# Deeper load buffers, stores held back, and arithmetic spread over three engines in a residual layer normalization

## The chip, the cores and the metric

The kernel runs on one core of a Trainium2 chip. The metric is the device time of one execution in microseconds (us). The profile names the core's engines: DVE is the vector engine, ACT the scalar engine, Pool the general engine, and SyncE (SP in the profile) only issues transfers here. "SPq", "POOLq" and "DVEq" are the queues or sequencers of those engines. DMA stands for the core's 16 transfer engines. The *span* is the time from the first to the last instruction in the profile; the time is about 1.7 to 2 us longer.

## The reference

```python
x, residual: (16, 1024, 512) float32; gamma, beta: (512,); eps = 1e-5

z = x + residual
mean = np.mean(z, axis=-1, keepdims=True)
var = np.var(z, axis=-1, keepdims=True)
return gamma * (z - mean) / np.sqrt(var + eps) + beta
```

There are 16384 rows of 512 numbers. With 128 rows to a tile that is 128 tiles. Two inputs of 33.55 MB are read and one output of 33.55 MB is written, and nothing is used twice, so nearly all of the 101.02 MB on the profile's page is unavoidable.

## The kernel before

The rows are worked on in 39 chunks: a head of 1, 1 and 2 tiles, 28 chunks of 4 tiles, and a tail of 2, 2, 2, 2, 1, 1, 1, 1 tiles. All loads are issued by SyncE and all stores by Pool, which also converts from fp16 to fp32. There are three buffers for X and three for R.

```python
LOAD_BUFS = 3
WORK_BUFS = 4
...
for ci, ns in enumerate(chunks):
    ...
    X = loads.tile([P, ns * D], FP32, name="X", tag="X")
    R = loads.tile([P, ns * D], FP32, name="R", tag="R")
    x_dma_eng.dma_start(out=X, in_=xs)                 # SyncE
    r_dma_eng.dma_start(out=R, in_=rs)                 # SyncE
    ...
    for j in range(ns):                                # Z = X + R, sz = its sum, on DVE
        nc.vector.tensor_tensor_reduce(out=Z3[:, j, :], in0=X3[:, j, :], in1=R3[:, j, :],
            ..., op0=OP.add, op1=OP.add, accum_out=sz[:, j : j + 1])
    for j in range(ns):                                # sq = sum of squares, on ACT
        nc.scalar.activation(out=sqd, in_=Z3[:, j, :], func=AF.Square,
            accum_out=sq[:, j : j + 1])
    nc.scalar.activation(out=msq, in_=sz, func=AF.Square, scale=inv_D)
    nc.vector.scalar_tensor_tensor(out=vr, in0=sq, scalar=inv_D, in1=msq, ...)
    nc.scalar.activation(out=rstd, in_=vr, func=AF.Sqrt, bias=eps_t)
    nc.vector.reciprocal(out=rstd, in_=rstd)
    nc.scalar.activation(out=nm, in_=sz, func=AF.Identity, scale=-inv_D)
    for j in range(ns):                                # normalize, times gamma, plus beta: all DVE
        nc.vector.tensor_scalar(out=W3[:, j, :], in0=Z3[:, j, :], scalar1=nm[...], scalar2=rstd[...], ...)
        nc.vector.tensor_tensor(out=W3[:, j, :], in0=W3[:, j, :], in1=gamma_b, op=OP.mult)
        nc.vector.tensor_tensor(out=W3[:, j, :], in0=W3[:, j, :], in1=beta_b, op=OP.add)
    nc.gpsimd.dma_start(out=os_, in_=W)                # Pool
```

## Time and profile before

| what | before |
|---|---|
| time, median of 16 runs | 256.96 us (256.57 to 258.44) |
| span of the profiled run | 255.1 us |
| DVE, ACT, Pool busy | 215.3, 106.4, 22.1 us |
| transfer rate, 20 to 215 us | 423 GB/s |
| bytes moved after 215 us | 11.98 MB in 40.1 us |

First the page of the kernel before. The line of digits gives DVE's busy share in tenths in 40 equal slices of the span, and the line below it the GB/s of those slices.

```profile
span 255.1 us, 1456 instructions
...
DVE 215.3 (84%) x720; ACT 106.4 (42%) x375; POOL 22.1 (9%) x45
...
DVE  1577799998889899778979878898887889999972
...
GB/s 148 399 421 416 421 425 423 425 424 421 423 425 418 429 420 424 425 421 424 420 423 429 420 424 424 421 429 419 425 427 421 423 426 385 407 384 403 347 129 123
...
```

The reader should see a flat middle at 420 to 425 GB/s in which DVE is *not* full (mostly 7 to 9 tenths), and then an end that falls off: the last two slices move 129 and 123 GB/s. The next fence is the table of stretches: start and end, length, the busy time of each engine (with the number of instructions), the granted clock, the DMA share and GB/s.

```profile
...
core 0: us, DVE busy (x) ACT busy (x) POOL busy (x), PEclk, DMA share, GB/s
20.00:215.00 195.00, 172.08 (x571) 82.31 (x286) 13.29 (x25) 1.00 1.09 423
215.00:240.00 25.00, 24.76 (x88) 13.19 (x50) 3.19 (x6) 1.00 1.04 380
240.00:244.10 4.10, 2.79 (x12) 2.30 (x10) 0.53 (x1) 1.00 0.87 307
244.10:255.10 11.00, 5.37 (x18) 1.39 (x6) 2.12 (x4) 1.00 0.39 111
...
```

From 20 to 215 us the transfers are the limit. From 215 to 240 us DVE is: it is busy for 24.76 of 25 us, and the rate falls to 380 GB/s. The waits of SyncE's queue from 215 to 245 us say what the loads wait for (what waited, on what; us in total, times, longest; L99 is line 99 of that kernel):

```profile
...
SPq L99 <- DVE W L144: 16.9, 5, 4.8
SPq L99 <- DVE sz L118: 9.9, 1, 9.9
SPq L99 <- DVE rstd L140: 1.8, 1, 1.8
```

The loads wait for DVE to free one of the three buffers. After the last load has landed (244.1 us), the rest is arithmetic on the last chunks and their stores, at 111 GB/s over 11 us.

### The profile page before, as it was taken

The page shows a single profiled execution, that of the slowest core. Times are in us where ns is not written, and L with a number is a line of the kernel's source. Part 1 is how long each engine was busy: PE and PEld are TensorE (multiplying, and loading weights), DVE is VectorE, ACT ScalarE, POOL GpSimd, SP SyncE. Part 2 cuts the span into 40 slices and gives each one's busy share as a digit, 9 for nine tenths or more (in the row PEclk, how much of TensorE's full clock was granted, in tenths as well). Part 3 has the DMA queues.
Part 4 walks back from the last instruction along what each step waited for, and adds up shares of the span by engine and source line. Part 5 has one row for each costly group of instructions (what it writes and reads, how often), then busy time and mean ns, then how long its engine had stood idle before and what let it go on. Part 6 is the DMA issues. An engine that isn't in the chain of part 4 may idle for free.

```text
span 255.1 us, 1456 instructions
## 1 busy us (share of the span) xinstructions
DVE 215.3 (84%) x720; ACT 106.4 (42%) x375; POOL 22.1 (9%) x45
## 2 busy tenths in 40 slices
DVE  1577799998889899778979878898887889999972
ACT  4133545352724335253332624334272333545530
POOL 2010000100000000000000000000000000011121
DMA  5999999999999999999999999999999999999944
GB/s 148 399 421 416 421 425 423 425 424 421 423 425 418 429 420 424 425 421 424 420 423 429 420 424 424 421 429 419 425 427 421 423 426 385 407 384 403 347 129 123
DMA packets 17147, 101.02 MB, mean 396 GB/s; under 512 B 1904, under 2 KB 2160, under 8 KB 6384
## 3 DMA queue, kind: packets, MB, share of 16 engines
q1 hardware_dynamic: 11232, 67.11, 68.7%
q0 software_dynamic: 5904, 33.82, 34.8%
q14 instruction: 11, 0.09, 0.1%
HBM read 67.63 MB, written 33.55 MB: 397 GB/s over the span
## 4 chain that ended last, share of the span: by engine, by line
DMA 52%; DVE 30%; issue 9%; ACT 5%; POOL 1%; SPq 1%; POOLq 0%; DVEq 0%; ACTq 0%
DMA R<-in_residual_dram 52%; DVE Z L118 10%; DVE W L144 7%; DVE W L152 6%; DVE W L155 5%; ACT sqd L129 4%; POOL out_dram L159 1%; SPq L99 1%; DVE rstd L140 1%; DVE sz L118 1%; DVE vr L136 1%; ACT rstd L139 0%; POOLq L192 0%; SPq L100 0%; ACT nm L141 0%
## 5 line engine op out<-in xcount | busy, mean ns | idle before, releaser
L129 ACT ACTIVATE sqd<-Z 128x512 f16<-128x512 f16 x128 | 79.7, 623 | 94.1 <-DVE sz L118 92.8
L118 DVE CUSTOM_DVE_ANT_0 Z<-X,R 128x512 f16<-128x512 f32 x128 | 84.4, 684 | 27.7 <-DMA R<-in_residual_dram 27.7
L152 DVE TENSOR_TENSOR W<-W,gamma_b 128x512 f16<-128x512 f16 x128 | 48.6, 422 | 0.1
L155 DVE TENSOR_TENSOR W<-W,beta_b 128x512 f16<-128x512 f16 x128 | 48.6, 422 | 0.1
L144 DVE TENSOR_SCALAR W<-Z,nm,rstd 128x512 f16<-128x512 f16 x128 | 47.3, 411 | 0.2
L159 POOL DMA_DIRECT2D out_dram<-W x39 | 20.7, 532 | 227.6 <-DVE vr L136 119.7
L139 ACT ACTIVATE rstd<-vr,eps_t 128x4 f32<-128x4 f32 (+2 forms) x39 | 11.3, 294 | 46.3 <-DVE vr L136 46.0
L129 ACT ACTIVATION_READ_ACCUMULATOR sqd<-Z 128x1 f32 x128 | 23.9, 186 | 0.0
L118 DVE DVE_READ_ACCUMULATOR2_ANT sz<- 128x1 f32 x128 | 10.9, 85 | 0.0
L136 DVE SCALAR_TENSOR_TENSOR vr<-sq,msq 128x4 f32<-128x4 f32 (+2 forms) x39 | 6.0, 159 | 4.5 <-ACT sqd L129 3.6
L140 DVE RECIPROCAL rstd<-rstd 128x4 f32<-128x4 f32 (+2 forms) x39 | 6.6, 171 | 1.4 <-ACT rstd L139 1.4
L135 ACT ACTIVATE msq<-sz 128x4 f32<-128x4 f32 (+2 forms) x39 | 7.4, 190 | 0.0
L141 ACT ACTIVATE nm<-sz 128x4 f32<-128x4 f32 (+2 forms) x39 | 7.3, 188 | 0.0
L88 ACT ACT_TABLE_LOAD x1 | 1.3, 1283 | 0.7 <-PEq L178 0.7
L85 DVE MEMSET eps_t<- 128x1 f32 x1 | 0.1, 59 | 0.8 <-PEq L178 0.8
L82 POOL DMA_DIRECT2D gamma_b<-in_gamma_dram x1 | 0.7, 667 | 0.8 <-PEq L192 0.8
L83 POOL DMA_DIRECT2D beta_b<-in_beta_dram x1 | 0.5, 540 | 0.0
L88 ACT ACTIVATE zero_t<-zero_t 128x1 f32<-128x1 f32 x1 | 0.2, 203 | 0.0
L178 POOL MEMSET const-float32-0.0<- 128x1 f32 x1 | 0.1, 98 | 0.2 <-issue 0.2
L178 POOL MEMSET const-bfloat16-1.0<- 128x1 bf16 x1 | 0.1, 101 | 0.0
L178 POOL MEMSET const-float32-1.0<- 128x1 f32 x1 | 0.1, 98 | 0.0
L178 POOL MEMSET const-uint8-127<- 128x1 uint8 x1 | 0.1, 98 | 0.0
(1 smaller groups left out, 0.1 us busy)
## 6 DMA issues: line engine op xcount, KB each, us to landing
X<-in_x_dram SPq DMA_DIRECT2D x28, 1024.0 KB, 11.4
R<-in_residual_dram SPq DMA_DIRECT2D x28, 1024.0 KB, 15.8
out_dram<-W POOLq DMA_DIRECT2D x28, 1024.0 KB, 9.3
X<-in_x_dram SPq DMA_DIRECT2D x5, 512.0 KB, 7.3
R<-in_residual_dram SPq DMA_DIRECT2D x5, 512.0 KB, 8.2
out_dram<-W POOLq DMA_DIRECT2D x5, 512.0 KB, 5.2
X<-in_x_dram SPq DMA_DIRECT2D x6, 256.0 KB, 5.1
R<-in_residual_dram SPq DMA_DIRECT2D x6, 256.0 KB, 5.4
```

The source lines that it names most:

```text
L99: x_dma_eng.dma_start(out=X, in_=xs)
L118: nc.vector.tensor_tensor_reduce(out=Z3[:, j, :], in0=X3[:, j, :], in1=R3[:, j, :], scale=1.0, scalar=0.0, op0=OP.add, op1=OP.add, accum_o ...
L129: nc.scalar.activation(out=sqd, in_=Z3[:, j, :], func=AF.Square, accum_out=sq[:, j : j + 1],)
L135: nc.scalar.activation(out=msq, in_=sz, func=AF.Square, scale=inv_D)
L136: nc.vector.scalar_tensor_tensor(out=vr, in0=sq, scalar=inv_D, in1=msq, op0=OP.mult, op1=OP.subtract)
L139: nc.scalar.activation(out=rstd, in_=vr, func=AF.Sqrt, bias=eps_t)
L140: nc.vector.reciprocal(out=rstd, in_=rstd)
L141: nc.scalar.activation(out=nm, in_=sz, func=AF.Identity, scale=-inv_D)
L144: nc.vector.tensor_scalar(out=W3[:, j, :], in0=Z3[:, j, :], scalar1=nm[:, j : j + 1], scalar2=rstd[:, j : j + 1], op0=OP.add, op1=OP.mult,)
L152: nc.vector.tensor_tensor(out=W3[:, j, :], in0=W3[:, j, :], in1=gamma_b, op=OP.mult)
L155: nc.vector.tensor_tensor(out=W3[:, j, :], in0=W3[:, j, :], in1=beta_b, op=OP.add)
L159: nc.gpsimd.dma_start(out=os_, in_=W)
```

## The change

Its intent is to keep the transfers full to the end. Three things change:

1. Six load buffers in place of three, so that loads need not wait for DVE.
2. Finished chunks are held back: up to five chunks stay in SBUF before their store is issued (`STORE_LAG = 5`, twelve W buffers). When the loads are done there are stores left to issue, and the arithmetic of the last chunks can run beside them.
3. Arithmetic is taken off DVE. The odd tiles of a chunk are normalized on ACT (61 of 128), and the statistics of the 31 head and bulk chunks are computed on Pool, with a power of -0.5 for the root. The order on DVE, ACT and Pool is written out by hand, with each chunk's second half after the first half of the next chunk.

The diff, cut to its core:

```diff
-LOAD_BUFS = 3
+LOAD_BUFS = 6
+W_BUFS = 12
+STORE_LAG = 5
+BULK_ON_POOL = True
+ZNORM = "split"
...
+        if on_pool:
+            nc.gpsimd.tensor_scalar(out=nm, in0=sz, scalar1=-inv_D, ..., op0=OP.mult)
+            nc.gpsimd.tensor_tensor(out=t0, in0=nm, in1=nm, op=OP.mult)
+            nc.gpsimd.tensor_scalar(out=t1, in0=sq, scalar1=inv_D, scalar2=eps, ...)
+            nc.gpsimd.tensor_tensor(out=t1, in0=t1, in1=t0, op=OP.subtract)
+            nc.gpsimd.tensor_tensor(out=rstd, in0=t1, in1=nhalf_t[:, :ns], op=OP.pow)
+            nc.gpsimd.tensor_tensor(out=bb, in0=nm, in1=rstd, op=OP.mult)
+        else:
+            nc.scalar.activation(out=t0, in_=sz, func=AF.Square, scale=inv_D)
+            # on Pool, so that the stores queued behind it keep pace with the loads
+            nc.gpsimd.tensor_scalar(out=nm, in0=sz, scalar1=-inv_D, ..., op0=OP.mult)
...
+    def stage_b_act(c):                      # odd tiles of a chunk
+            nc.scalar.activation(out=W3[:, j, :], in_=Z3[:, j, :], func=AF.Identity,
+                scale=rstd[:, j : j + 1], bias=bb[:, j : j + 1])
...
-        nc.gpsimd.dma_start(out=os_, in_=W)
+        for ci, ns in enumerate(chunks):
+            bulk = ci < n_bulk
+            full = len(held) >= (1 if bulk and BULK_ON_POOL else 2)
+            ...
+            new = stage_a(ns, bulk and BULK_ON_POOL)
+            ...
+            if full:
+                stage_b_dve(held.pop(0))
+            held.append(new)
+            store(max(0, len(pending) - STORE_LAG))
+        store(len(pending))
```

More of the change, by code (lines that the diff above doesn't have):

```diff
@@ L16 @@
 TAIL = [2, 2, 2, 2, 1, 1, 1, 1]
-LOAD_BUFS = 3
+LOAD_BUFS = 6
 WORK_BUFS = 4
-HALF = True
-X_DMA = "sync"
-R_DMA = "sync"
-OUT_DMA = "pool"
+W_BUFS = 12
+STORE_LAG = 5
+BULK_ON_POOL = True
+ZNORM = "split"
 @with_exitstack
@@ L65 @@
     assert sum(chunks) == n_tok_tiles
-    HT = FP16 if HALF else FP32
     consts = ctx.enter_context(tc.tile_pool(name="consts", bufs=1))
@@ L72 @@
     stats = ctx.enter_context(tc.tile_pool(name="stats", bufs=6))
-    dma_engines = {"act": nc.scalar, "sync": nc.sync, "pool": nc.gpsimd}
-    out_dma_eng = dma_engines[OUT_DMA]
-    x_dma_eng = dma_engines[X_DMA]
-    r_dma_eng = dma_engines[R_DMA]
-    gamma_b = consts.tile([P, D], HT)
-    beta_b = consts.tile([P, D], HT)
-    gb_load = nc.gpsimd if HALF else nc.sync
-    gb_load.dma_start(out=gamma_b, in_=gamma[None, :].to_broadcast((P, D)))
-    gb_load.dma_start(out=beta_b, in_=beta[None, :].to_broadcast((P, D)))
+    gamma_b = consts.tile([P, D], FP16)
+    beta_b = consts.tile([P, D], FP16)
+    nc.gpsimd.dma_start(out=gamma_b, in_=gamma[None, :].to_broadcast((P, D)))
+    nc.gpsimd.dma_start(out=beta_b, in_=beta[None, :].to_broadcast((P, D)))
     eps_t = consts.tile([P, 1], FP32)
@@ L87, with stage_a @@
     nc.vector.memset(zero_t, 0.0)
+    nhalf_t = consts.tile([P, NS_BULK], FP32)
+    nc.vector.memset(nhalf_t, -0.5)
     nc.scalar.activation(out=zero_t, in_=zero_t, func=AF.Sqrt)
     row0 = 0
-    for ci, ns in enumerate(chunks):
+    def stage_a(ns, on_pool):
+        nonlocal row0
         xs = xf[row0 : row0 + P * ns].rearrange("(p j) d -> p (j d)", j=ns)
@@ L98 @@
         R = loads.tile([P, ns * D], FP32, name="R", tag="R")
-        x_dma_eng.dma_start(out=X, in_=xs)
-        r_dma_eng.dma_start(out=R, in_=rs)
+        nc.sync.dma_start(out=X, in_=xs)
+        nc.sync.dma_start(out=R, in_=rs)
         X3 = X.rearrange("p (j d) -> p j d", d=D)
         R3 = R.rearrange("p (j d) -> p j d", d=D)
-        Z = work.tile([P, ns * D], HT, name="Z", tag="Z")
+        Z = work.tile([P, ns * D], FP16, name="Z", tag="Z")
         Z3 = Z.rearrange("p (j d) -> p j d", d=D)
-        W = work.tile([P, ns * D], HT, name="W", tag="W")
+        W = work.tile([P, ns * D], FP16, name="W", tag="W", bufs=W_BUFS)
         W3 = W.rearrange("p (j d) -> p j d", d=D)
-        sqd = work.tile([P, D], HT, name="sqd", tag="sqd", bufs=2)
+        sqd = work.tile([P, D], FP16, name="sqd", tag="sqd", bufs=2)
         sz = stats.tile([P, ns], FP32, name="sz", tag="sz")
         sq = stats.tile([P, ns], FP32, name="sq", tag="sq")
-        msq = stats.tile([P, ns], FP32, name="msq", tag="msq")
-        vr = stats.tile([P, ns], FP32, name="vr", tag="vr")
         rstd = stats.tile([P, ns], FP32, name="rstd", tag="rstd")
         nm = stats.tile([P, ns], FP32, name="nm", tag="nm")
+        bb = stats.tile([P, ns], FP32, name="bb", tag="bb")
+        t0 = stats.tile([P, ns], FP32, name="t0", tag="t0")
+        t1 = stats.tile([P, ns], FP32, name="t1", tag="t1")
         for j in range(ns):
@@ L134 @@
             )
-        nc.scalar.activation(out=msq, in_=sz, func=AF.Square, scale=inv_D)
-        nc.vector.scalar_tensor_tensor(
-            out=vr, in0=sq, scalar=inv_D, in1=msq, op0=OP.mult, op1=OP.subtract
-        )
-        nc.scalar.activation(out=rstd, in_=vr, func=AF.Sqrt, bias=eps_t)
-        nc.vector.reciprocal(out=rstd, in_=rstd)
-        nc.scalar.activation(out=nm, in_=sz, func=AF.Identity, scale=-inv_D)
-        for j in range(ns):
+        c = dict(ns=ns, W=W, W3=W3, Z3=Z3, nm=nm, rstd=rstd, bb=bb, os_=os_,
+                 t0=t0, t1=t1, sq=sq)
@@ new lines, in stage_a @@
+        if on_pool:
+            nc.gpsimd.tensor_scalar(
+                out=nm, in0=sz, scalar1=-inv_D, scalar2=None, op0=OP.mult
+            )
+            nc.gpsimd.tensor_tensor(out=t0, in0=nm, in1=nm, op=OP.mult)
+            nc.gpsimd.tensor_scalar(
+                out=t1, in0=sq, scalar1=inv_D, scalar2=eps, op0=OP.mult, op1=OP.add
+            )
+            nc.gpsimd.tensor_tensor(out=t1, in0=t1, in1=t0, op=OP.subtract)
[3 more added lines that the diff above has]
+            nc.scalar.activation(out=t0, in_=sz, func=AF.Square, scale=inv_D)
+            nc.gpsimd.tensor_scalar(
+                out=nm, in0=sz, scalar1=-inv_D, scalar2=None, op0=OP.mult
+            )
@@ new lines, in stage_a, with stats_var, stats_root @@
+        c["var_done"] = c["root_done"] = on_pool
+        return c
+    def stats_var(c):
+        if not c["var_done"]:
+            c["var_done"] = True
+            nc.vector.scalar_tensor_tensor(
+                out=c["t1"], in0=c["sq"], scalar=inv_D, in1=c["t0"],
+                op0=OP.mult, op1=OP.subtract,
+            )
+            nc.scalar.activation(out=c["rstd"], in_=c["t1"], func=AF.Sqrt, bias=eps_t)
+    def stats_root(c):
+        if not c["root_done"]:
+            c["root_done"] = True
+            nc.vector.reciprocal(out=c["rstd"], in_=c["rstd"])
+            if split_js(c["ns"])[0]:
+                nc.vector.tensor_tensor(
+                    out=c["bb"], in0=c["nm"], in1=c["rstd"], op=OP.mult
+                )
@@ new lines, in split_js @@
+    def split_js(ns):
+        act_js = [j for j in range(ns) if ZNORM == "split" and j % 2 == 1]
+        return act_js, [j for j in range(ns) if j not in act_js]
+    def stage_b_act(c):
+        ns, W3, Z3, rstd, bb = (c[k] for k in ("ns", "W3", "Z3", "rstd", "bb"))
+        for j in split_js(ns)[0]:
+            nc.scalar.activation(
+                out=W3[:, j, :],
+                in_=Z3[:, j, :],
+                func=AF.Identity,
+                scale=rstd[:, j : j + 1],
+                bias=bb[:, j : j + 1],
+            )
@@ L144, with stage_b_dve @@
+    def stage_b_dve(c):
+        ns, W, W3, Z3, nm, rstd, os_ = (
+            c[k] for k in ("ns", "W", "W3", "Z3", "nm", "rstd", "os_")
+        )
+        act_js, dve_js = split_js(ns)
+        for j in dve_js:
             nc.vector.tensor_scalar(
@@ L151 @@
             )
+        for j in act_js + dve_js:
             nc.vector.tensor_tensor(
@@ L154 @@
             )
+        for j in act_js + dve_js:
             nc.vector.tensor_tensor(
@@ L157, with store @@
             )
-        if HALF:
-            nc.gpsimd.dma_start(out=os_, in_=W)
-        else:
-            out_dma_eng.dma_start(out=os_, in_=W)
+        pending.append((os_, W))
+    pending = []
+    ET = mybir.EngineType
+    n_bulk = len(head) + (sum(chunks) - sum(head) - sum(tail)) // ns_bulk
+    with tc.manual_schedule(engines={ET.DVE, ET.Activation, ET.Pool}):
+        def store(n):
+            for _ in range(min(n, len(pending))):
+                o, w = pending.pop(0)
+                nc.gpsimd.dma_start(out=o, in_=w)
+        held = []
+        for ci, ns in enumerate(chunks):
+            bulk = ci < n_bulk
+            full = len(held) >= (1 if bulk and BULK_ON_POOL else 2)
+            if held:
+                stats_var(held[-1])
+            if full:
+                stats_root(held[0])
+                stage_b_act(held[0])
+            new = stage_a(ns, bulk and BULK_ON_POOL)
+            if held:
+                stats_root(held[-1])
+            if full:
+                stage_b_dve(held.pop(0))
+            held.append(new)
+            store(max(0, len(pending) - STORE_LAG))
+        store(len(pending))
+        for c in held:
+            stats_var(c)
+        for c in held:
+            stats_root(c)
+            stage_b_act(c)
+            stage_b_dve(c)
+            store(len(pending))
 _INS = ['x', 'residual', 'gamma', 'beta', 'eps']
```

## The prediction

> **What bounds it now.** The transfers. In the stretch table, 20 to 215 us moves 423 GB/s, DMA share 1.09, DVE busy 172.1 of 195 us: slack in DVE, none in the queues. 101.02 MB (the page) at that rate are 238.8 us; the span is 255.1. About 4 us is the head (2.1 us before the first bytes, then 364 GB/s until 20 us). About 12 us is the tail: from 215 us on 11.98 MB take 40.1 us instead of 28.3. (a) From 215 to 240 us DVE is busy 24.8 of 25 us and SyncE's loads wait for DVE to free one of three buffers; the rate falls to about 380 GB/s. (b) The last R lands near 244.3 us; the remaining 10.8 us are arithmetic and 0.7 MB of transfers.
>
> **What the change does.** Bytes and queues are the same, so the steady stretch cannot get faster. It
> - doubles the load buffers, so that loads no longer wait for DVE in the tail;
> - keeps five finished chunks back, so that 2.6 MB of stores (the last seven chunks) are left when the last load lands. The tail's arithmetic runs beside them;
> - moves 61 of 128 normalizations (411 ns) from DVE to ACT, and the statistics of 31 chunks to Pool. DVE: 215 - 61x0.33 (pipelined) - 31x0.33 = about 185 us. ACT: 106 + 61x0.7 - 31x0.5 = about 133 us. Neither bounds beside 239.
>
> **The risk in the middle.** ACT waits for Pool's root before its normalizations, and only then squares the next chunk. That loop is 3.1 us of squares, 1.4 us of normalizations and Pool's four dependent steps (scale, subtract, power, product). A chunk's transfers take 3.15 MB / 423 GB/s = 7.4 us, so Pool may take 2.9 us. The trace has no Pool arithmetic. The Trainium skill, "SBUF — State Buffer", section "Who interferes with whom", says DVE with two SBUF inputs and a GpSimd instruction that reads SBUF lock each other out for a whole instruction; no run shows it here yet. I guess 2 to 3 us: it just fits. At 4 us, 28 chunks would each lose about 1 us.
>
> **Time.** Head: 4 us as before. Before the first store, near 25 us, there are only loads; the Trainium skill, "DMA: Bandwidth & Descriptors", section "SWDGE vs HWDGE vs iDMA", measured 408.7 GB/s for a load stream, so perhaps 1 us is lost; this trace has no such stretch. All but about 3 MB is moved at about 236 us, when the last R lands. Then 9 us: 1.3 us until Pool may issue, 2.6 MB of stores (6.5 us), receipt. Span near 245.5, plus the 1.7 us that the time has over the span: 247.2 us. The gain, 3.8%, is in the tail. Range 243.8 to 251.5. Faster by over 2%: 0.87; within 2%: 0.10; slower: 0.03.
>
> **What would show it.** Right: 20 to 215 us still at 420 to 425 GB/s; DVE busy near 185 us, ACT near 133; last R landing at 234 to 238 us; the page's last two slices well above 123 GB/s; few DVE pieces in the chain of waits after 215 us. Wrong: a middle under 415 GB/s, ACT waiting on Pool, or an unchanged last landing and 10 us of tail.
>
> **What would make it wrong.** Pool's arithmetic slow or locked out by DVE; stores alone slower than mixed traffic, so that 2.6 MB take 10 us; stores falling over five chunks behind.

## The result, and the profile after

| what | before | after |
|---|---|---|
| time, median | 256.96 us (16 runs) | 253.19 us (10 runs, 252.89 to 253.88) |
| span of the profiled run | 255.1 us | 251.2 us |
| DVE, ACT, Pool busy | 215.3, 106.4, 22.1 us | 196.9, 139.7, 116.9 us |
| rate, 20 to 215 us | 423 GB/s | 421 GB/s |

The ratio is 0.9844, with a 95% interval of 0.9827 to 0.9861. A ratio here is the mean time of one kernel's fast runs over that of the other's of the same rounds, so it isn't quite the ratio of the medians. The change saves 1.6%. The predicted 247.2 us and its range (243.8 to 251.5) are missed by 6.0 and 1.7 us. The page after:

```profile
span 251.2 us, 1521 instructions
...
DVE 196.9 (78%) x602; ACT 139.7 (56%) x335; POOL 116.9 (47%) x239
...
GB/s 159 399 420 423 417 423 423 412 425 419 421 420 424 425 424 424 417 425 427 419 419 430 424 417 424 428 420 419 423 427 421 415 421 422 408 421 429 265 302 205
...
L179 ACT ACTIVATE W<-Z,bb,rstd 128x512 f16<-128x512 f16 x61 | 46.5, 806 | 74.5 <-POOL bb L144 74.5
...
L143 POOL TENSOR_TENSOR rstd<-t,nhalf_t 128x4 f32<-128x4 f32 (+2 forms) x31 | 40.3, 1300 | 2.4
...
```

The two groups of instructions at the end of the fence are the new work that matters below: a normalization on ACT takes 806 ns on average, the root on Pool 1300 ns. The middle is as before, and the slices before the end are now full (421, 429 GB/s). Then come 265, 302 and 205. The stretches of the kernel after:

```profile
...
20.00:30.00 10.00, 9.02 (x29) 4.51 (x12) 7.86 (x9) 1.00 1.01 419
20.00:215.00 195.00, 166.82 (x501) 119.16 (x280) 99.57 (x194) 1.00 1.08 421
236.20:240.50 4.30, 2.29 (x8) 1.06 (x4) 1.35 (x3) 1.00 0.13 42
240.50:248.70 8.20, 2.23 (x7) 0.05 (x1) 3.29 (x7) 1.00 1.22 384
248.70:251.20 2.50, 0.00 (x0) 0.00 (x0) 0.00 (x0) 1.00 0.00 0
...
```

For 4.3 us in the middle of the end, from 236.2 to 240.5 us, nearly nothing moves: 42 GB/s. Then the stores that were held back run, until 248.7 us, and the span ends 2.5 us later. A finer view of the same time, the transfers of 228 to 252 us in 40 slices of 0.6 us, shows what kind of standstill it is:

```profile
...
DMA  9999999999999731000109999999999999000000
GB/s 416 416 427 440 413 406 427 430 345 427 427 420 440 253 109 41 27 27 27 41 27 423 410 430 437 410 430 417 423 379 410 406 403 239 0 0 0 0 0 0
...
```

The rate falls by steps to 27 GB/s and stays there for 3 us. 27 is one sixteenth of 430: *one* of the 16 transfer engines is still working while fifteen have nothing to do. The chain that ended last and the waits after 235 us say what it was working on and who waited for it (start, length, what; and: us in total, times, longest):

```profile
...
217.89 20.11 DMA R<-in_residual_dram
...
238.14 0.14 DVE Z L115
...
238.84 0.09 DVE rstd L166
...
239.01 0.28 POOL nm L148
...
239.44 0.58 POOL out_dram L218
...
```

```profile
...
POOL nm L148 <- DVE rstd L166: 6.0, 1, 6.0
...
DVE Z L115 <- DMA R<-in_residual_dram: 4.9, 1, 4.9
...
```

The last R landed at 238.0 us. DVE had waited 4.9 us for it. Pool then had to compute the last chunk's `nm` (6.0 us of waiting) before it got to the eight stores that stood behind that instruction in its program, although the data of most of them had long been ready. SyncE's queue, which in the kernel before waited 28.6 us for DVE in the last part, now waits for none of the compute engines there:

```profile
...
SPq L95 <- DMA X<-in_x_dram: 2.5, 1, 2.5
SPq L96 <- DMA R<-in_residual_dram: 0.9, 1, 0.9
```

The trace also holds the sixteen landings of each transfer, one for each engine. This list, worked out from it, gives the landings of four of the last transfers in us:

```
transfer                 first   8th     15th    16th
R of chunk 39 (last)     223.82  224.50  227.95  238.01
store of chunk 30        233.54  234.27  235.32  238.20
store of chunk 31        236.44  236.70  237.75  240.48
store of chunk 39 (last) 248.49  248.57  248.65  248.74
```

Fifteen engines had landed their part of the last R by 228.0 us; the sixteenth needed until 238.0. While loads and stores are both queued, a late engine's lag shows magnified in the loads; in the stores just before the standstill it is 2.7 to 2.9 us (15th to 16th).

### Where the predicted 6 us went

The prediction's sum for the end was: last R at 236, then 9 us. Term by term (the 1.2 us in the fourth row is what its 9 us leave after the other two):

| term | predicted | measured | difference |
|---|---|---|---|
| last R lands | 236 | 238.0 | +2.0 |
| until stores flow | 1.3 | 2.5 (to 240.5) | +1.2 |
| the stores left | 6.5 (2.6 MB) | 8.2 (3.15 MB: eight stores, twelve tiles) | +1.7 |
| last landing to the end of the span | 1.2 | 2.5 | +1.3 |

The terms sum to 245.0 predicted and 251.2 measured; the difference is 6.2 us, of which half a microsecond had been rounded up (the prediction wrote 245.5). All four can be read from traces. Two of them could have been read *before* the run: in the kernel before, the last store lands at 252.57 us and the span ends at 255.1, the same 2.5 us; and the last loads of that kernel have their sixteenth landing 1.5 to 2.1 us after their fifteenth (the last R: 242.65 and 244.14).

### The profile page after: what moved, and what is told of

Read it like the earlier page. It is cut to its first block, busy times and chain, and to the rows that moved or that the text cites. A ratio compares the mean times of both kernels' runs of the same rounds, so it can differ in the third digit from the quotient of the medians.

```text
span 251.2 us, 1521 instructions
## 1 busy us (share of the span) xinstructions
DVE 196.9 (78%) x602; ACT 139.7 (56%) x335; POOL 116.9 (47%) x239
## 2 busy tenths in 40 slices
DMA packets 17148, 101.03 MB, mean 402 GB/s; under 512 B 1904, under 2 KB 2160, under 8 KB 6384
## 4 chain that ended last, share of the span: by engine, by line
DMA 58%; POOL 13%; issue 8%; ACT 8%; DVE 7%; SPq 2%; POOLq 0%; DVEq 0%
DMA R<-in_residual_dram 58%; POOL rstd L143 6%; DVE W L202 5%; ACT sqd L126 4%; ACT W L179 4%; POOL t L142 2%; DVE Z L115 2%; POOL out_dram L218 1%; POOL t L138 1%; SPq L95 1%; POOL t L139 1%; POOL bb L144 1%; SPq L96 1%; DVE W L206 0%; POOLq L274 0%
## 5 line engine op out<-in xcount | busy, mean ns | idle before, releaser
L115 DVE CUSTOM_DVE_ANT_0 Z<-X,R 128x512 f16<-128x512 f32 x128 | 81.4, 686 | 17.0 <-DMA R<-in_residual_dram 17.0
L179 ACT ACTIVATE W<-Z,bb,rstd 128x512 f16<-128x512 f16 x61 | 46.5, 806 | 74.5 <-POOL bb L144 74.5
L139 POOL TENSOR_SCALAR t<-sq 128x4 f32<-128x4 f32 (+2 forms) x31 | 6.8, 219 | 84.7 <-ACT sqd L126 84.6
L143 POOL TENSOR_TENSOR rstd<-t,nhalf_t 128x4 f32<-128x4 f32 (+2 forms) x31 | 40.3, 1300 | 2.4
L193 DVE TENSOR_SCALAR W<-Z,nm,rstd 128x512 f16<-128x512 f16 x67 | 25.0, 409 | 8.9 <-POOL rstd L143 8.8
L218 POOL DMA_DIRECT2D out_dram<-W x39 | 24.2, 621 | 0.8
L142 POOL TENSOR_TENSOR t<-t,t 128x4 f32<-128x4 f32 (+2 forms) x31 | 14.6, 471 | 2.6
L138 POOL TENSOR_TENSOR t<-nm 128x4 f32<-128x4 f32 (+2 forms) x31 | 13.3, 428 | 2.6
L135 POOL TENSOR_SCALAR nm<-sz 128x4 f32<-128x4 f32 (+2 forms) x31 | 8.1, 260 | 11.1 <-DVE sz L115 10.3
L144 POOL TENSOR_TENSOR bb<-nm,rstd 128x4 f32<-128x4 f32 (+2 forms) x31 | 7.0, 225 | 2.4
```

What stands on the lines that cost most here:

```text
L138: nc.gpsimd.tensor_tensor(out=t0, in0=nm, in1=nm, op=OP.mult)
L139: nc.gpsimd.tensor_scalar(out=t1, in0=sq, scalar1=inv_D, scalar2=eps, op0=OP.mult, op1=OP.add)
L142: nc.gpsimd.tensor_tensor(out=t1, in0=t1, in1=t0, op=OP.subtract)
L143: nc.gpsimd.tensor_tensor(out=rstd, in0=t1, in1=nhalf_t[:, :ns], op=OP.pow)
L144: nc.gpsimd.tensor_tensor(out=bb, in0=nm, in1=rstd, op=OP.mult)
L179: nc.scalar.activation(out=W3[:, j, :], in_=Z3[:, j, :], func=AF.Identity, scale=rstd[:, j : j + 1], bias=bb[:, j : j + 1],)
```

## The experiments

Fifteen kernels were run. All but the probe were timed in five rounds against the kernel before, on the same chip in the same call, and all gave correct results. The kernel of the change itself ran again only in the third call (e9), so elsewhere it is compared by the two ratios to the kernel before. The first three calls used one chip and the fourth another; the medians of the kernel before were 257.14 (first call), 257.64 (second and third) and 256.93 us (fourth). Where a text uses a letter for a theory, its numbers say what the theory commits to; here the theories are named in words:

- *Late engine*: one of the 16 transfer engines falls behind during the run, and the end waits for it.
- *Arithmetic*: the arithmetic moved to Pool and ACT holds back the end or the middle.
- *Order of the stores*: the stores stand behind Pool's wait for the last sum, and that order costs the time.
- *Fetches*: the engine is late because instruction fetches share it. Later, its narrower form: the fetches of DVE's program land on one engine.
- *Start*: the engines are already apart a few microseconds into the run, and the fetches add little.

### First call: the parts of the change one at a time

**e1: the six buffers alone, in the kernel before.**

```diff
-LOAD_BUFS = 3
+LOAD_BUFS = 6
```

> The kernel before with six load buffers instead of three and nothing else. Theory A (the loss of before lies in its tail, where DVE is full and the loads wait for buffers; deeper buffers let the loads run ahead, but the arithmetic after the last load stays): 20 to 215 us at 420 to 425 GB/s, time 254.5 to 256.5, up to 1% faster than before. Rival B (buffers are all that the change needed): 253 to 253.5, as the changed kernel. Rival C (the loads were never held by buffers): 256.7 to 257.2.

Measured: 256.26 us, ratio 0.9964 (0.9941 to 0.9988). The loads stop waiting for DVE, but DVE's work is then simply the end: after 240 us it is still busy for 4.7 of 5 us, and the last slices are 298, 135 and 122 GB/s. Buffers alone are worth 0.4%.

**e2: the change without held stores.**

```diff
-STORE_LAG = 5
+STORE_LAG = 0
```

> The changed kernel with no finished chunk held back (lag 0 instead of 5). Theory A (holding stores back only moves bytes to behind the last landing; what counts is how long the transfer engines stand still in the tail): the last R lands later, about 240 to 243 us, fewer stores (3 instead of 8) are issued after it, and the time is within 2.5 us of 253.2, most likely 1 to 2 us longer. Rival B (the held stores are the gain): the time goes back to 256 to 257.

Measured: 255.55 us (254.64 to 257.6), ratio 0.9948 (0.9911 to 0.9984), against 0.9844 with stores held. The last R lands at about 243.4 us: the stores compete with the loads to the last, and nothing is left to run beside the last arithmetic. The runs are spread widely, but holding the stores back is worth around 1%.

**e3: the change without the moved arithmetic.**

```diff
-BULK_ON_POOL = True
-ZNORM = "split"
+BULK_ON_POOL = False
+ZNORM = "dve"
```

> The changed kernel with all arithmetic back on DVE and ACT: no statistics on Pool, no normalization on ACT. Theory A (the middle is bound by transfers in either form, so moving arithmetic there is worth nothing): 20 to 205 us at 420 to 425 GB/s, time within 1.5 us of 253.2, the rest from a fuller DVE in the tail. Rival B (Pool's slow root and its lock-out by DVE cost time in the changed kernel): faster than 253.2 by over 1 us. Rival C (the offload is where the gain came from): 255.5 or more.

Measured: 253.33 us (253.24 to 256.04), ratio 0.9869 (0.983 to 0.9908); the interval holds the 0.9844 of the whole change. DVE is back at 214.2 us and the middle still runs at 421 GB/s. So the largest part of the diff, the moved arithmetic, is worth nothing that these runs can show, and the *arithmetic* theory falls: without any of it the miss is the same. The end looks different, however:

```profile
span 252.6 us, 1498 instructions
...
DVE 214.2 (85%) x721; ACT 109.2 (43%) x336; POOL 35.4 (14%) x84
...
GB/s 148 389 423 422 416 420 420 418 419 424 422 422 427 420 422 423 420 427 420 420 425 424 422 424 419 425 423 427 419 422 423 413 422 414 421 366 372 401 398 14
...
```

There is no standstill here, and the time is the same. From the landings: each of the last nine stores has its sixteenth landing 3.5 to 3.6 us after the fifteenth; the last one has its fifteenth at 246.56 and its sixteenth at 250.13 us. The same lateness that is a standstill in one kernel is a ragged end in the other.

**e4: the change with three load buffers.**

```diff
-LOAD_BUFS = 6
+LOAD_BUFS = 3
```

> The changed kernel with three load buffers instead of six. Theory A (depth lets fifteen of sixteen transfer engines run ahead of a lagging one and lets the loads run ahead of DVE in the tail): the loads of the tail wait for buffers, but the last R of the lagging engine lands less far behind the others; time 253.5 to 256. Rival B (depth is the whole gain): 256 or more. Rival C (depth only lengthens the lag): faster than 253.2.

Measured: 257.53 us, ratio 1.0008 (0.9984 to 1.0032): all of the gain is gone. It is lost in the first hundred microseconds, as the stretches show:

```profile
...
20.00:60.00 40.00, 34.33 (x104) 22.56 (x53) 21.93 (x38) 1.00 0.97 382
60.00:100.00 40.00, 34.44 (x103) 25.30 (x60) 19.03 (x40) 1.00 1.07 402
100.00:215.00 115.00, 95.20 (x285) 68.68 (x159) 59.21 (x110) 1.00 1.09 420
...
```

In this kernel SyncE waits 138.0 us for DVE's sums. The new order lets DVE start a chunk's Z only after other work, so a buffer is held longer, and three are too few. Put together: buffers alone 0.4%, held stores and moved arithmetic with three buffers 0%, buffers and held stores without moved arithmetic 1.3%, everything 1.6%. The deeper buffers and the held stores need each other. (e3 keeps the hand-written order of the instructions, which no run here tests by itself.)

### Second call: is it one engine, and do fetches make it late?

**e5: which engine is it?** Sixteen small loads of the first k rows (k = 1 to 16) are issued before the 37th chunk.

```diff
+            for k in range(1, 17):
+                t = consts.tile([P, D], FP32, ...)
+                nc.sync.dma_start(out=t[:k], in_=xf[:k])
```

> The changed kernel with sixteen tiny extra loads queued behind the loads of the third-last chunk; the k-th uses k rows, so that it uses k transfer engines. In the changed kernel fifteen of the sixteen landings of each late load come together and the sixteenth up to 10 us later. Theory A (it is one and the same engine): from some k on every tiny load lands 5 us or more later than the ones below k, and k names the engine. Rival (the late one changes from load to load): no such step. Time about 1 us longer, not of interest.

The Trainium skill, "DMA: Bandwidth & Descriptors", section "Why a DMA increments its semaphore by 16 and not by 1", says that a transfer is spread over k of the engines, k by its outermost dimension, that each counts the semaphore up as its part lands, and that a SyncE transfer takes the lowest-numbered k. The trace agrees with the first part (k landings). Landings in us:

```
k=1: 216.49
k=2: 219.06 220.49
k=3: 221.55 222.26 223.02
k=4: 221.75 222.45 223.38 225.95
k=5: 221.92 221.93 222.63 223.56 227.25
k=6: ...                       225.78 227.95
k=7: ...                       228.32 230.68
k=8: ...                       228.50 230.87
```

Up to k = 3 no landing stands more than 1.5 us off; from k = 4 on, exactly one is 2.2 to 3.7 us behind the rest (k = 9: 228.67 and 231.05; k = 10: 230.88 and 233.31). The step is there, but smaller than the 5 us expected. With the page's rule it is the fourth engine. The *late engine* theory stands: it is the same single engine each time. The one time of this kernel (255.22 us) means nothing; it does more work.

**e6: more fetches, on an engine that has nothing else to do.**

```diff
+    for _ in range(512):
+        nc.tensor.matmul(pe_out, pe_in, pe_in)
```

> The changed kernel with 512 one-element matmuls (1024 instructions) on the TensorE, which nothing waits for: 8 more instruction fetches of 8 KB. Theory A (all instruction fetches ride on one transfer engine at about 0.31 us each, 11 of them in the changed kernel make its lag of 3.6 us, and the loads' completion waits for it): the lag at the end grows to about 6 us, the last R lands about 2.5 us or more later, time 255.2 to 257. Rival B (the one engine is slow by itself, fetches don't matter): 253 to 253.5 and the same lag.

Measured: 251.77 us (251.01 to 253.5), ratio 0.9792 (0.9758 to 0.9825). The slowdown that the *fetches* theory expected (255.2 to 257) did not come, although more fetches did. The page shows them as a queue of their own (queue, kind: packets, MB, share of 16 engines):

```profile
...
q14 instruction: 12, 0.10, 0.1%
q8 instruction: 4, 0.07, 0.1%
...
```

The twelve of q14 are in the kernel of the change too. The four of q8 are new: 16384 bytes each, 64 for each of the 1024 instructions, in the trace at 6.4, 12.5, 18.5 and 24.4 us and 0.93 us long. Here are the landings of two loads, one from before the second of them and one from after the last (the first landing in us, and the sixteen distances from it; the first fetch falls in the unsteady start):

```
 9.89: 0.00 0.12 0.23 0.38 0.68 0.75 0.77 0.87 0.97 1.11 1.11 1.13 1.42 1.44 1.49 1.55
27.07: 0.00 0.11 0.21 0.34 0.62 0.87 1.08 1.11 1.12 1.42 1.43 1.44 1.54 2.18 2.22 2.42
```

Three engines, at 0.75, 0.77 and 0.97, have moved to 2.18, 2.22 and 2.42: three fetches set three *different* engines back by about 1.45 us each, and the kernel is not slower for it. So the theory falls in its wide form, in which all fetches ride on one engine. What is left is a narrower one: only those fetches cost time that hit the engine that ends last. That the kernel is, if anything, a little *faster* is not explained; the six runs of e6 themselves differ by 2.5 us.

**e7: fewer instructions on DVE.** The two loops over a chunk's tiles become one instruction each; DVE's counted instructions fall from 602 to 424.

```diff
-        for j in act_js + dve_js:
-            nc.vector.tensor_tensor(out=W3[:, j, :], in0=W3[:, j, :], in1=gamma_b, op=OP.mult)
+        nc.vector.tensor_tensor(out=W3, in0=W3, op=OP.mult,
+            in1=gamma_b[:, None, :].to_broadcast((P, ns, D)))
         (the same for beta)
```

> The changed kernel with gamma and beta applied to a whole chunk by one instruction each instead of one for each tile: 178 fewer DVE instructions, so 1 or 2 fewer fetches, and DVE less busy. Theory A (lag grows by 0.31 us for each fetch): 0.3 to 0.8 us faster than 253.2. Rival B (DVE and Pool's lock-out matter in the middle): over 1 us faster. Rival C (neither): 253 to 253.5.

Measured: 251.74 us (250.96 to 253.28), ratio 0.979 (0.9755 to 0.9825), a larger gain than the 0.3 to 0.8 us expected. By its size it fits the expectation's rival B as well (over 1 us, from DVE and Pool keeping each other out in the middle); but from 20 to 215 us this kernel moves 422 GB/s and the kernel after 421, so the gain is not in the middle, where B has it. There is no standstill (last slices 403, 414, 110 GB/s), and the last engine is 1.1 us behind the fifteenth in the stores instead of 2.7 to 2.9. That distance is not quite like for like: the late engine began 0.3 us after the first in both profiled runs, but here three others began 2.0 to 2.3 us after it, and 1.4 at most in the kernel after. As DVE is also less busy here (185.6 us), e7 alone does not separate fewer instructions from less work; e11 and e13 do.

**e8: the stores issued ahead of Pool's wait for the last sum.**

```diff
+            if ci == len(chunks) - 1:
+                store(len(pending))
             new = stage_a(ns, ...)
```

> The changed kernel with the five held stores issued before Pool waits for the last chunk's sum instead of after. In the changed kernel the transfer engines stand nearly still from 236.2 to 240.5 us, because the held stores queue behind that wait. Theory A (the lagging engine shares its queue turns between the stores and its remaining loads, so the stores fill the gap but make its last load land later): the gap is gone, the last R lands at 241 to 243 us instead of 238, and the time is within 1 us of 253.2. Rival B (the gap is the loss): 249 to 251.

Measured: 253.04 us (252.56 to 253.26), ratio 0.9824 (0.9798 to 0.9849). The order is mended for the last chunk only. Stores flow again at about 237.2 us instead of 240.5, but the gap is not gone: from 234.8 to 237.2 us only 26 GB/s move, since Pool now stands behind the sum of chunk 38, whose R lands at 234.65 us. The last R lands at 238.79 us, and not at 241 to 243. The gain is only about half a microsecond by the ratios (0.9844 and 0.9824), and the intervals overlap. The landings suggest why: the last store of this kernel has its fifteenth landing at 248.06 and its sixteenth at 248.78 us, against 248.65 and 248.74 in the kernel of the change. The fifteen engines come 0.6 us sooner; the late one comes at the same time. So the *order of the stores*, as far as this edit mends it, does not explain the miss; a kernel whose stores never stand behind such a sum was not run. The standstill is fifteen engines that wait for one, and giving the fifteen something to do doesn't help the one, which has its own sixteenth of the stores still to move.

### Third call: what makes the engine late?

**The pattern.** In the first 45 us there are only loads, and the sixteen landings of successive loads keep their distances to a few hundredths of a microsecond. What changes them are the instruction packets of 8192 bytes, 0.31 us each, in the trace at 30.3, 44.5, 46.4, 74.2, 112.2, 123.6, 147.4, 165.7, 175.6, 189.7 and 214.8 us (and a twelfth in the standstill, at 239.9). Landings of four loads of the kernel after, first landing in us and the sixteen distances from it:

```
27.41: 0.00 0.08 0.09 0.13 0.14 0.15 0.17 0.26 0.46 0.48 0.62 0.70 0.73 0.94 1.24 1.42
32.40: 0.00 0.06 0.09 0.12 0.13 0.14 0.17 0.46 0.47 0.63 0.71 0.72 0.93 1.23 1.23 1.42
67.21: 0.00 0.05 0.07 0.11 0.14 0.46 0.47 0.60 0.68 0.73 0.77 0.79 0.93 1.22 1.23 1.41
74.67: 0.00 0.05 0.06 0.09 0.12 0.46 0.47 0.60 0.69 0.70 0.75 0.76 0.91 1.19 1.37 1.94
```

Between the first two lines lies the fetch at 30.3 us: one engine, at 0.26, is now at 1.23. The others stand still. The fetches at 44.5 and 46.4 us move two *other* engines (two of the low values go to about 0.8). At 74.2 us the engine at 1.23 moves again, to 1.94. The packets at 30.3 and 74.2 us thus hit one and the same transfer engine, and each packet sets its engine back by 0.6 to 1.0 us. In e8 it is again one engine that moves twice, from 0.86 to 1.83 at 30.8 us and from 1.80 to 2.76 at 74.5.

Whose program? 8192 bytes are 128 instructions of 64 bytes (the Trainium skill, "GPSIMD Engine Reference", section 2.1, "Instruction dispatch", speaks of "the 64-byte instruction"; the 65536 bytes that e6 fetched for 1024 instructions agree). When the packets at 30.3, 74.2, 123.6, 165.7 and 214.8 us come, DVE has run 67, 184, 323, 443 and 583 of its 676 recorded instructions: 129 apart on average. In e7, with 531, the packets at 31.5, 95.9, 159.4 and 219.9 us come 131 of DVE's instructions apart, and the other six stand within 1.1 us of their times in the kernel after. So these five, and four, are the fetches of DVE's program. Five fetches at 0.97 + 4 x 0.7 us put an engine that starts at 0.27 us at 4.0, which is about 2.6 us behind the next one at 1.4: about the 2.7 to 2.9 us seen in the stores at the end. This is an estimate from two jumps that were read, since after 75 us stores mix with the loads and the jumps can no longer be read one by one.

**e9: the kernel of the change once more.**

> The changed kernel unaltered, beside the next three. In its trace, 253.2 us, fifteen engines have no data left at 236 us and one goes on to 240 us; that one had fallen back by 0.97 us at a DVE instruction fetch near 30 us and by about 0.7 us at each later one. Expect 253 to 253.5, with the same: one jump at each of the fetches near 31 and 75 us of the same engine.

Measured: 253.74 us (252.36 to 254.1), ratio 0.984 (0.9809 to 0.987). The same picture: the last R's sixteenth landing is at 237.28 us, with its fifteenth at 228.7; the engine jumps at 30.8 us from 1.72 to 2.70 and again at 74.7. What differs from one run to the next is where the engine starts: 0.26 us after the first in one, 1.72 in this one. This distance arises within the first 9 us. It may be one reason for the spread of 1 to 2 us among runs of a kernel; with one trace for each kernel that is not shown.

**e10: more instructions on DVE, first try.** Fourteen memsets of one element a row, on one tile, are added to each bulk chunk.

```diff
+        if ns == NS_BULK:
+            for _ in range(14):
+                nc.vector.memset(pad_t[:, :1], 0.0)
```

> The changed kernel with 14 one-element memsets of 59 ns on DVE in each of 28 bulk chunks: 392 more DVE instructions, so 3 more fetches of DVE's program, and 0.84 us more DVE time a chunk, which DVE has. Theory A (each fetch of DVE's program holds up the same transfer engine by 0.7 us, and the loads and the end wait for it): the last engine's lag at the end grows by about 2 us and the time by 1.5 to 3 us over the unaltered kernel of the same call. Rival B (fetches don't set the time): as the next kernel.

Measured: 262.57 us, ratio 1.0199 (1.0167 to 1.0232), and void as a test of fetches. As they write the same place, the memsets waited for each other: 1.70 us per fourteen. The loop of DVE, ACT and Pool then took 7.51 us for a chunk, more than its transfers at 7.4, the loads lost their lead, and SyncE ended up waiting for DVE:

```profile
...
SPq L96 <- DVE pad_t L195: 156.5, 26, 6.9
...
```

What it does show is how narrow the loop's margin is: in the kernel after, one turn takes 7.03 us (33.91 to 40.94 us).

**e11: the same busy time in one instruction (the control).**

```diff
+            nc.vector.memset(pad_t, 0.0)          # 128 x 800, 0.725 us
```

> The control for the one before: the same DVE time as one memset of 800 elements in each bulk chunk, 28 instructions more instead of 392. Both theories: within 0.5 us of the unaltered kernel of the same call. If it is as slow as the padded kernel, DVE's time and not its fetches was the cause.

Measured: 252.33 us (251.98 to 254.46), ratio 0.9811 (0.9774 to 0.9848): no slowdown, and with 1.4 us under e9 more than the 0.5 us of difference expected. Another 0.7 us of DVE time per chunk (209.9 us busy in all) costs nothing.

**e12: gamma and beta without 256 small transfers.** The rows of gamma and beta are loaded once and spread to 128 partitions by a matmul with ones.

```diff
-    nc.gpsimd.dma_start(out=gamma_b, in_=gamma[None, :].to_broadcast((P, D)))
+        nc.scalar.dma_start(out=row, in_=vec[None, :])
+        nc.tensor.matmul(spread, ones, row)
+        nc.vector.tensor_copy(out=full, in_=spread)
```

> The changed kernel with gamma and beta loaded as one row each and spread over the partitions by a matmul, instead of by two loads that read the same row for each of 128 partitions. In the changed kernel the landings of one load are 0.2 us apart before those two loads and 1.4 to 2.6 us apart after them, and 5 to 10 us moves 333 GB/s. Theory A (those loads cost about 1 us of everybody's time and the apartness): offsets stay under 0.4 us until the first fetch near 30 us, 5 to 10 us moves over 400 GB/s, time 0.7 to 1.5 us shorter than the unaltered kernel. Rival B (only the slowest engine counts, and it started among the first): offsets small but time within 0.5 us.

Measured: 250.97 us (250.54 to 251.28), ratio 0.9743 (0.9715 to 0.9772), 2.8 us below e9, more than the 0.7 to 1.5 expected. The reason given beforehand failed: the distances between engines after 8 us were still 1.4 us and not under 0.4. The *start* differences thus don't come from these small transfers. From 5 to 10 us, 392 GB/s moved, against 333 in the kernel after and over 400 expected. What the profile does show is a better first 12 us, here in this kernel and then in the kernel after:

```profile
...
3.00:12.00 9.00, 3.63 (x4) 1.01 (x4) 6.29 (x16) 2.89 (x8) 4.73 (x15) 1.00 1.01 371
...
```

```profile
...
3.00:12.00 9.00, 3.07 (x8) 1.44 (x4) 3.27 (x11) 1.00 0.99 329
...
```

42 GB/s over 9 us are 0.38 MB, and 0.26 MB less had to be moved at all (100.77 against 101.03 MB). Together 0.64 MB, at 423 GB/s 1.5 us; that is an estimate from these numbers. The other 1.3 us were not isolated, and a spread of 1 to 2 us among runs could hold them.

### Fourth call: the deciding pair, and a better kernel

By then the prediction's miss was sized, but whether DVE's fetches cause the late engine had only been argued from timing and landings: e6 had added fetches to other engines, and e10 was void.

**e13: more instructions on DVE that don't wait for each other.** The same fourteen memsets, each on its own tile: 392 more instructions.

```diff
+    pads = [consts.tile([P, 1], FP32, ...) for i in range(14)]
...
+            for t in pads:
+                nc.vector.memset(t, 0.0)
```

> The changed kernel with 14 one-element memsets in each of 28 bulk chunks, each into a tile of its own, so that none waits for another: 392 more DVE instructions, 3 more fetches of DVE's program, at most 0.8 us more DVE time a chunk (a single memset of 0.73 us in the same place did not slow the kernel: e11). Theory A (each fetch of DVE's program holds up the same transfer engine by about 0.7 us): that engine ends about 2 us later than in the unaltered kernel, in the trace the gap between it and the fifteenth grows from 3.3 to 5 us or more, and the time is 1.5 to 3 us over the 253.2 to 253.7 us of the unaltered kernel. Rival B (the engine is slow by itself, or by the stores): 252 to 254 us and the same gap.

Measured: 254.95 us (254.28 to 256.19), ratio 0.9917 (0.9892 to 0.9943). That is about 1.9 us slower than the kernel of the change (0.984 of 256.93), although fourteen memsets now take only 0.22 us, DVE's busy time rises only from 196.9 to 202.0 us, and e11 with 209.9 us lost nothing. The page:

```profile
span 253.0 us, 1913 instructions
...
DVE 202.0 (80%) x994; ACT 139.9 (55%) x335; POOL 114.1 (45%) x239
...
GB/s 156 385 424 425 413 425 425 414 420 422 424 421 422 425 422 426 421 420 429 417 427 420 420 425 421 425 421 426 422 418 420 420 416 416 421 426 255 258 414 173
...
q14 instruction: 15, 0.12, 0.1%
...
```

The middle is as fast as ever; the standstill (255, 258) is what grew. There are 15 instruction packets in place of 12: DVE's program now shows eight fetches during the run (26.5, 52.7, 81.2, 109.5, 137.1, 161.3, 187.0 and 217.8 us) instead of five. The first two move the same engine, from 0.46 to 1.4 and from there to 2.4 us behind the first. In the loads that begin to land between 150 and 215 us, the sixteenth landing comes 6.0 us after the fifteenth (median), against 4.1 in e9, 2.6 in the profiled run of the kernel after, and 2.7 in the control e11. That distance alone does not tell the time: it holds the engine's start as well, which differs by more than a microsecond, and e3 has 5.0 without being slower. The time, from six runs against eleven of the kernel before, averages over the starts.

One part of the expectation did not come: the last R lands no later (238.09 us, and 238.01 in the kernel after). But the two R before it do, at 232.96 and 236.76 us instead of 225.35 and 231.05. So Pool gets past the sums of chunks 37 and 38 only at 233.97 and 237.76 us instead of 228.47 and 232.06, and when the last R has landed nine stores of 4.19 MB are yet to be issued, instead of eight of 3.15 MB. At 420 GB/s the difference is 2.5 us, an estimate.

More instructions on DVE, hardly more work: a late engine that is further behind and a longer time. Together with its control, and with e6, in which fetches that hit other engines cost nothing, this run supports the *fetches* theory in its narrow form. What stays argued is the step from the two fetches whose effect can be read to the six later ones.

**e14: e7 and e12 together.**

> The changed kernel with both gains at once: gamma and beta applied to a chunk by one instruction each (e7), and spread by a matmul instead of being loaded 128 times (e12). Theory A (fetches and loads are separate costs on the same engines): gains add, 248.5 to 250 us. Rival (they hit the same engine time): 250.5 to 251.5 us, as e12 alone.

Measured: 249.82 us (249.31 to 251.06), ratio 0.9719 (0.9693 to 0.9746). It beats both kernels, the one before by 2.8%.

```profile
span 247.7 us, 1392 instructions
...
PE 3.7 (2%) x4; PEld 1.1 (0%) x4; DVE 186.8 (75%) x427; ACT 139.7 (56%) x335; POOL 110.4 (45%) x237
...
GB/s 236 409 423 423 418 419 419 415 423 421 421 423 423 423 423 422 423 422 423 423 423 423 423 423 423 421 423 423 421 426 423 415 421 416 410 417 417 407 412 67
...
```

There is no standstill: 407 to 417 GB/s in the last slices until 241 us, and then 67. The last store has its fifteenth landing at 243.82 and its sixteenth at 245.27 us. Of the span's last 3.9 us, 1.45 are still a late engine and 2.4 the ending after the last landing. Against the kernel of the change (0.984 in e9, on the other chip) it is 1.2% by the two ratios.

**e15: e14 with the stores ahead of Pool's wait, as in e8.** The edits are those of e7, e8 and e12.

> As e14, and the held stores issued before Pool waits for the last chunk's sum (e8). With a shorter lag the stores no longer delay the last load by as much as they fill: 0.5 to 1.5 us faster than e14, the gap before the last stores gone. If the lag still sets the end: as e14 within 0.4 us.

Measured: 249.92 us, ratio 0.9718 (0.9691 to 0.9745), the same as e14. Where there is no standstill, there is nothing for that order to save.

## Why the prediction was wrong

**Right: what bounds the kernel.** The middle held at 421 GB/s (420 to 425 foreseen). The loads no longer wait for DVE. The last two slices are 302 and 205, far above 129 and 123. Almost no DVE piece is left in the chain after 215 us. Fifteen of the sixteen engines had done their part by 236.2 us, where the prediction had everything moved at 236.

**Right, and rightly called a guess: Pool's four dependent steps.** 2 to 3 us were guessed; in the chunk at 35.48 us they take from 35.48 to 37.99 us, and the loop just fits. The mechanism that made it a risk is visible too. The Trainium skill, "SBUF — State Buffer", section "Who interferes with whom", says that a DVE instruction with two SBUF inputs and a Pool instruction that reads SBUF keep each other out. Here is one Pool instruction of one shape at two times, in the timeline of the kernel after (start, length, engine, line, operation):

```profile
...
19.54 0.22 POOL L138 TENSOR_TENSOR t<-nm 128x4 f32<-128x4 f32 x1
```

```profile
...
24.52 3.49 POOL L138 TENSOR_TENSOR t<-nm 128x4 f32<-128x4 f32 x1
24.58 1.43 DVE L202 TENSOR_TENSOR W<-W,gamma_b 128x512 f16<-128x512 f16 x4
...
25.92 1.43 DVE L206 TENSOR_TENSOR W<-W,beta_b 128x512 f16<-128x512 f16 x4
...
27.27 0.69 DVE L115 CUSTOM_DVE_ANT_0 Z<-X,R 128x512 f16<-128x512 f32 x1
...
```

It took 0.22 us at 19.54 and 3.49 us at 24.52, while DVE ran multiplications and additions with two inputs back to back and then Z. The trace agrees with the page, and shows more: as no DVE instruction here takes over 0.69 us, Pool was kept out over several in a row. No run here took the lock away by itself, so how much of Pool's 116.9 us is waiting is open.

**Wrong: "All but about 3 MB is moved at about 236 us, when the last R lands."** The first half held and the second did not. A load has landed when its *last* engine has landed, and one engine was 2 us later than the mean rate says (238.0). The prediction had treated 16 engines as one pipe.

**Wrong: "Then 9 us: 1.3 us until Pool may issue, 2.6 MB of stores (6.5 us), receipt."** It took 13.2 us. Every term was too small: 2.5 us until the stores flowed, because DVE's Z, a read of its sum and Pool's `nm` come in between and the first store takes time to issue; 8.2 us for 3.15 MB, because the store of chunk 32 also stood behind Pool's wait; and 2.5 us from the last landing to the end, which the kernel before shows as well. The late engine is behind the first of the four differences and behind the standstill (mending the order of the stores alone gave about half a microsecond, e8); how much of the second and third it also carries was not separated. The last difference, 1.3 us, has nothing to do with it: it is a constant that was misread.

**Wrong, without effect: the busy times.** DVE fell by 18.4 us rather than 30, and ACT rose by 33.3 us rather than 27 (a normalization on ACT took 806 ns, and 700 were taken for it). Neither engine was the limit.

**Not foreseen: the moved arithmetic is worth nothing measurable** (e3). The prediction had put the gain on buffers and held stores, so its sum does not depend on it, but it did not say that the largest part of the diff could be left out.

**"Stores alone slower than mixed traffic", a named risk, did not come true.** Once flowing, stores alone ran at about 420 GB/s; the 384 GB/s of the stretch include starting and ending.

What stays open: why a packet that takes 0.31 us sets its engine back by 0.6 to 1.0 us; what sets the engines 1.4 to 2.1 us apart in the first 9 us (e12 excludes the small transfers as its main cause); why e6 was a little faster than the unaltered kernel; and 1.3 us of e12's gain.

## What to carry to other kernels

When transfers are the limit, the end of a kernel is set by the slowest of the sixteen engines and not by bytes over mean rate: look at the fifteenth and the sixteenth landing of the last transfers before predicting, and read constants such as the time from the last landing to the end from the trace you have. The number of instructions can matter more than busy time: 392 more on DVE, with 5 us more of busy time, cost about 1.9 us (e13), while 28 more with 13 us of it cost nothing (e11), and moving 18 us of arithmetic off DVE brought nothing (e3). Two instructions in the place of eight, and two rows spread without 256 small transfers, together brought 249.82 us. And count packets of every size before calling a test void: e6's four stood in its page under another queue. Deeper load buffers and held stores need each other, so test such parts alone and together.

## What the Trainium skill lacked or had wrong

- "Runtime: NRT & Kernel Launch", section "Instruction fetch mechanics", says that a sequencer fetches its program by its own DMA queue in blocks of 16 KiB and that the cost is "mostly hidden". TensorE's four packets in e6 have these 16384 bytes; those of the other programs are 8192 here, and each sets one of the engines that carry the kernel's data back by 0.6 to 1.0 us (for DVE 0.26 to 1.23 and 1.23 to 1.94 in the distances above). With 392 more DVE instructions a transfer-bound kernel lost about 1.9 us (e13). No page says which transfer engine a fetch falls on: DVE's hit the same one each time that could be read, three of TensorE's hit three different ones (e6).
- "DMA: Bandwidth & Descriptors", section "Latency and other measured facts", calls engines 7 and 15 the ones that are usually slower. Here it was the fourth, number 3 when counted from 0, by the rule of the lowest-numbered engines (e5: the late landing appears with k = 4, 225.95 against 223.38 us), and fewer or more DVE instructions changed how late it was (e7, e13).
- The same page, section "SWDGE vs HWDGE vs iDMA", has 408.7 GB/s for a stream of loads; the loads alone ran at 419 GB/s here (20 to 30 us of the kernel after), and loads and stores together at 421 to 423. The limit of about 358 GB/s for one core with HBM (the page's section "Where 436 GB/s comes from") does not hold for a core that runs alone; other places of the skill say so.
- No page gives the time of Pool's small statistics: 128x4 elements took 219 to 471 ns for multiply, add and subtract and 1300 ns for the power (means in the kernel after, with DVE running beside it).
- No page has the 2.4 to 2.5 us from the last landing of a store to the end of the span (252.57 to 255.1 before, 248.74 to 251.2 after, 245.27 to 247.7 in e14).
